# A fused encoder layer: the SSM side chain starts four steps later, loads by SyncE's queue, and its splits stand elsewhere in VectorE's order

## The chip, the cores and the metric

One Trainium2 chip, one core. The metric is the device time of one execution in microseconds, on the slowest core (here the only one). The program is about 19,700 instructions, which each engine executes in the order in which the program was written; between engines there are semaphores.

## The reference, cut to what matters

The kernel computes one layer of a hybrid encoder for an input of 2048 x 1024 floats. The normalised input h is projected once into queries, keys, values, SSM inputs u and the gates of both branches. Branch A is windowed attention. Branch B is a bidirectional state space model: 32 groups of 16 channels with 64 complex states each. Both are projected, gated, summed and added to the input.

```python
h = rms_norm(x, norm_gain[l])
proj = jnp.einsum('bsd,de->bse', h, w_in[l])
q, k, v, z_attn, u_ssm, z_ssm, g = jnp.split(proj, SPLITS, axis=-1)
...
attn = windowed_gqa(q, k, v, attn_sink[l], rel_bias_table) * jax.nn.silu(z_attn)
y = s5_bidirectional(u_ssm, ssm_a_re[l], ssm_a_im[l], ssm_log_dt[l], ...)
...
# in s5_bidirectional, for each direction d:
a_bar = jnp.exp(lam * dt)
_, xs = lax.associative_scan(_scan_op, (a_el, bu), reverse=(d == 1), axis=0)
y = y + Re(xs) c_re - Im(xs) c_im
```

## The kernel before, in words

**Main stream.** TensorE multiplies h with the weights of the input projection, one key (128 output columns) and one block of 512 positions at a time. Numbers are held as a high and a low part, so `mm3` (L220 to L222) issues three matmuls of 128 x 512 for each of eight slices, 24 for one projection. The weights of a key come on SyncE's (SP's) queue into two buffers named raw; `split_w` (L157) has ScalarE round the high part wh (L163) and GpSimd subtract the low part wl in four pieces (L155), which frees the buffer for the next load. The stream goes through 25 keys for blocks 2 and 3, then three keys for all four blocks (there h of blocks 0 and 1 is read again from hS and split by ScalarE, hh L1263, and GpSimd, hl L1267), then 25 keys for blocks 0 and 1.

**Side chain.** Between these matmuls the program places the steps of one generator, `chain` (L1380): the SSM, then attention, then the preparation of the last stage. `turn` (L115) is called four times in a projection and takes as many steps from the chain as a credit allows, 2 x rate for one projection: RATE2 = 1.237 up to the second set of keys, RATE3 = 1.499 behind. So a step of the chain is a place in the order of every engine, some ten projection matmuls long.

**The SSM.** `ssm` (L669) works through eight frames of four groups. Ahead of them the start section (L986 to L1006) loads U, builds the first tables and the first matrices. In each `frame(i)` (L913) the order is fixed by hand, with tables and splits of frame i + 1 placed between steps of frame i:

- `mats` (L783): TensorE transposes the table wt (L796), ScalarE writes Wh (L799), VectorE Wl (L790). wt is made by `prep_w`, on GpSimd (L692 to L694 with `part`), and on VectorE for frame 0; `prep_e` makes the tables ec and es on GpSimd, three products each.
- `zmat` (L804): TensorE forms Z from the negated table wo (L821, negated by ScalarE L760) and writes a last piece (L828); VectorE adds the diagonal (L831). Z is stored to zS and loaded again as M by `load_m` (L838) in another layout; `split_m` splits it (L748 on ScalarE, L749 on VectorE).
- `inject` (L858): TensorE applies W to U, whose two halves come by `load_u` (L773) and are split by `split_u` (L748, L749).
- `rotate` (L867, L868, L870), `scan` (L879), rotate again: VectorE, the recurrence. Then `high_h` (ScalarE, Hh L886) and `low_h` (VectorE, Hl L891) split the state. This happens twice in a frame, for two halves.
- `emit` (L893): TensorE sums M times U (L901) and the table ws times H (L905). ScalarE evacuates Y (L909).
- `prep_o` (L729): the output table wo of the next frame, on VectorE: six operations (L692 to L694).

All loads of U and M are issued by ScalarE's queue (L773, L838), in order with ScalarE's other work.

## Time and profile before

| | us |
|---|---|
| runs of the kernel, median of 3 | 1507.56 (1506.02 to 1509.1) |
| the profiled execution | 1508.19 |
| its span | 1506.4 |
| TensorE busy in the span | 1418.1 (94%) |
| VectorE busy | 1041.8 (69%) |
| ScalarE busy | 659.9 (44%) |
| GpSimd busy | 637.9 (42%) |

The profile is one execution, recorded by the hardware. PE is TensorE, PEld its weight loads, DVE VectorE, ACT ScalarE, POOL GpSimd, SP SyncE; ACTq and SPq are the instructions by which these engines issue DMAs. A matmul's end is modelled, so gaps between starts tell more than durations. The clock that the page gives, PEclk, is the share of full speed granted to TensorE: 1.00 is 2.4 GHz, 0.50 is 1.2 GHz.

### The profile page before, as it was taken

The page shows a single profiled execution, that of the slowest core. Times are in us where ns is not written, and L with a number is a line of the kernel's source. Part 1 is how long each engine was busy: PE and PEld are TensorE (multiplying, and loading weights), DVE is VectorE, ACT ScalarE, POOL GpSimd, SP SyncE. Part 2 cuts the span into 40 slices and gives each one's busy share as a digit, 9 for nine tenths or more (in the row PEclk, how much of TensorE's full clock was granted, in tenths as well). Part 3 has the DMA queues.
Part 4 walks back from the last instruction along what each step waited for, and adds up shares of the span by engine and source line. Part 5 has one row for each costly group of instructions (what it writes and reads, how often), then busy time and mean ns, then how long its engine had stood idle before and what let it go on. Part 6 is the DMA issues. An engine that isn't in the chain of part 4 may idle for free.

```text
span 1506.4 us, 19697 instructions
## 1 busy us (share of the span) xinstructions
PE 1418.1 (94%) x6933; PEld 1154.6 (77%) x6933; DVE 1041.8 (69%) x1954; ACT 659.9 (44%) x1213; POOL 637.9 (42%) x683
## 2 busy tenths in 40 slices
PE   7999779899999999899999999999988999999998
PEld 6787567777778777788888888888766877877886
DVE  2327977779788788647999998874577386385442
ACT  6332133433534444535666666754453243242111
POOL 5520187758678777622111111112376153252320
PEclk9999989989999999999999999999999999999999
DMA  8534222322332332554333333235776375375441
GB/s 264 157 98 95 64 81 72 100 91 76 113 105 88 109 105 88 152 175 127 92 91 92 101 96 91 90 102 148 211 212 193 98 196 181 114 182 166 117 122 70
DMA packets 240723, 185.47 MB, mean 123 GB/s; under 512 B 57921, under 2 KB 202433, under 8 KB 240625
## 3 DMA queue, kind: packets, MB, share of 16 engines
q10 hardware_dynamic: 118192, 107.89, 24.3%
q1 hardware_dynamic: 122432, 76.34, 17.1%
q8 instruction: 54, 0.88, 0.2%
q14 instruction: 45, 0.36, 0.1%
HBM read 126.56 MB, written 57.62 MB: 122 GB/s over the span
## 4 chain that ended last, share of the span: by engine, by line
PE 39%; DVE 26%; issue 7%; DMA 6%; ACT 5%; POOL 4%; ACTq 1%; DVEq 0%; POOLq 0%; SPq 0%
PE pj L220 7%; PE pj L222 7%; PE pj L221 7%; PE s L1592 3%; PE s L1593 3%; PE s L1594 3%; DVE Hl L891 2%; DMA yt<-yS 2%; DVE X L879 2%; PE s L1163 2%; DVE X L868 2%; PE s L1110 2%; DVE rt L867 2%; DVE X L870 2%; PE s L1147 2%
## 5 line engine op out<-in xcount | busy, mean ns | idle before, releaser
L155 POOL TENSOR_TENSOR wl<-raw,wh 128x256 fp32r<-128x256 f32 x380 | 355.0, 964 | 573.5 <-ACT wh L163 483.7
L220 PE MATMUL pj<-hh,wh 128*128 128x512 f32 x976 | 391.2, 401 | 0.0
L222 PE MATMUL pj<-hh,wl 128*128 128x512 f32 x976 | 385.7, 395 | 0.0
L221 PE MATMUL pj<-hl,wh 128*128 128x512 f32 x976 | 385.6, 395 | 0.0
L222 PEld LDWEIGHTS pj<-hh,wl 128*128 128x128 f32 x976 | 185.6, 190 | 41.0
L220 PEld LDWEIGHTS pj<-hh,wh 128*128 128x128 f32 x976 | 186.3, 191 | 34.0
L221 PEld LDWEIGHTS pj<-hl,wh 128*128 128x128 f32 x976 | 186.1, 191 | 34.3
L163 ACT ACTIVATE wh<-raw 128x1024 fp32r<-128x1024 f32 x96 | 100.7, 1051 | 23.4 <-DMA raw<-in_w_branch_ssm_dram 7.9
L1592 PE MATMUL s<-woh,mh 128*128 128x512 f32 x256 | 102.3, 400 | 6.7 <-DVE xr L1599 6.7
L1594 PE MATMUL s<-woh,ml 128*128 128x512 f32 x256 | 102.0, 398 | 0.0
L1593 PE MATMUL s<-wol,mh 128*128 128x512 f32 x256 | 101.9, 398 | 0.0
L1127 ACT ACTIVATE p<-p,sml 128x384 f32<-128x384 f32 (+1 forms) x128 | 75.8, 594 | 16.3 <-DVE sml L1123 16.1
L1636 POOL TENSOR_TENSOR sm<-sm,mhalf 128x1 f32<-128x1 f32 x15 | 8.3, 550 | 170.1 <-DVE sm L1635 133.4
L404 ACT ACTIVATE st<-pj,bg 128x512 f32<-128x512 f32 x64 | 43.8, 685 | 79.0 <-PE pj L222 69.3
L1111 DVE CUSTOM_DVE_ANT_0 p<-s,bias 128x384 f32<-128x384 f32 (+1 forms) x128 | 68.3, 535 | 13.7 <-PE s L1110 13.2
L1599 DVE TENSOR_TENSOR xr<-xr,s 128x512 f32<-128x512 f32 x32 | 21.9, 686 | 69.3 <-PE s L1594 69.3
L867 DVE TENSOR_TENSOR rt<-X,es 128x1020 f32<-128x1020 f32 x32 | 43.3, 1353 | 38.1 <-issue 14.4
L1152 DVE TENSOR_TENSOR pl<-s,ph 128x512 fp32r<-128x512 f32 x92 | 62.9, 683 | 4.2 <-ACT ph L1150 2.9
L1110 PE MATMUL s<-kst,qs 128*128 128x384 f32 (+1 forms) x256 | 65.7, 339 | 0.0
L1592 PEld LDWEIGHTS s<-woh,mh 128*128 128x128 f32 x256 | 48.5, 189 | 20.5 <-DVE xr L1599 8.9
L870 DVE TENSOR_TENSOR X<-X,rt 128x510 f32<-128x510 f32 x64 | 62.0, 1009 | 1.1
L891 DVE TENSOR_TENSOR Hl<-X,Hh 64x1024 fp32r<-64x1024 f32 x32 | 46.7, 1460 | 17.9 <-ACT Hh L886 17.4
(307 smaller groups left out, 3049.2 us busy)
## 6 DMA issues: line engine op xcount, KB each, us to landing
raw<-in_w_in_dram SPq DMA_DIRECT2D x59, 512.0 KB
gS<-st ACTq DMA_DIRECT2D x64, 256.0 KB
gt<-gS ACTq DMA_DIRECT2D x64, 256.0 KB
x<-in_x_dram SPq DMA_DIRECT2D x16, 512.0 KB
raw<-in_w_branch_attn_dram SPq DMA_DIRECT2D x32, 256.0 KB
raw<-in_w_branch_ssm_dram SPq DMA_DIRECT2D x32, 256.0 KB
out_dram<-xr ACTq DMA_DIRECT2D x15, 512.0 KB
xr<-in_x_dram SPq DMA_DIRECT2D x12, 512.0 KB
```

Source lines behind the costliest of these rows:

```text
L155: eng.tensor_tensor(lo[:, ks], r[:, ks], hi[:, ks].bitcast(F32), ALU.subtract)
L163: A.activation(res[0], r, AF.Copy)
L220: PE.matmul(pt, w[0][:, k], r[0][:, k], start=start and k == 0, stop=False)
L221: PE.matmul(pt, w[0][:, k], r[1][:, k], start=False, stop=False)
L222: PE.matmul(pt, w[1][:, k], r[0][:, k], start=False, stop=stop and k == kt - 1)
L870: V.tensor_tensor(X[:, :, r], X[:, :, r], t[:, :, r], ALU.add if r == back else ALU.subtract)
L891: V.tensor_tensor(H[1][rows], xv, H[0][rows].bitcast(F32), ALU.subtract)
L1110: PE.matmul(pt[:, 0:w], s["qs"][:, h], kst[:, r, kv, k0 * 128:k1 * 128], start=r == 0, stop=r == 1)
L1127: A.activation(p[:, h, 0:w], p[:, h, 0:w], AF.Exp, bias=nm[:, j:j + 1], accum_out=den[:, j:j + 1])
L1592: PE.matmul(pt, mh[k][:, ts_], wo[0, n][:, k], start=k == 0, stop=False)
L1593: PE.matmul(pt, mh[k][:, ts_], wo[1, n][:, k], start=False, stop=False)
L1594: PE.matmul(pt, ml[k][:, ts_], wo[0, n][:, k], start=False, stop=k == KD - 1)
```

## The change

The chain waits four steps before it begins, and its start has further yields, so that the first transposes of `mats` come six steps later and the frames seven. U and M are loaded by SP's queue instead of ScalarE's, and M one step earlier. In a frame, M is split right after the first Hl, ahead of the rotation; both halves of the next U are split before the first `emit`, ahead of the second Hl; the six VectorE operations of `prep_o` come in two parts of three in two steps. The rate of the attention is 1.56 instead of 1.499. No arithmetic changes.

```diff
-RATE3 = 1.499
+RATE3 = 1.56
...
-        def prep_o(i, eng=Q):
-            raw_o[i] = [pool.tile(sh, F32, tag=f"wo{n}", name=f"wo{n}") for n in range(2)]
-            table(raw_o[i], i, wo_re, wo_im, cc_re, cc_im, eng)
+        def prep_o(i):
+
+            o = [pool.tile(sh, F32, tag=f"wo{n}", name=f"wo{n}") for n in range(2)]
+            pr, pi, qr, qi = bc(wo_re, i, 1), bc(wo_im, i, 1), bc(cc_re, i, 0), bc(cc_im, i, 0)
+            for n, (a, b, c, d, op) in enumerate(((pr, qr, pi, qi, ALU.subtract), (pr, qi, pi, qr, ALU.add))):
+                r = rtile().rearrange("p g r m -> p g (r m)")
+                t = [r[:, m].rearrange("p (g j c) -> p g j c", g=GB, c=C) for m in range(2)]
+                V.tensor_tensor(t[0], a, b, ALU.mult)
+                V.tensor_tensor(t[1], c, d, ALU.mult)
+                V.tensor_tensor(o[n], t[0], t[1], op)
+                if n == 0:
+                    yield
+            raw_o[i] = o
...
-                A.dma_start(out=raw[:, j], in_=chan(uS, i * GB + half * 2 + j))
+                nc.sync.dma_start(out=raw[:, j], in_=chan(uS, i * GB + half * 2 + j))
...
-                A.dma_start(
+                nc.sync.dma_start(
                     out=raw[:, g],
...
             yield from slot()
+            load_m(i)
             if nx:
                 next(ms)
             split_o(i)
             yield from slot()
-            load_m(i)
             high_h(i, 0)
...
             low_h(i)
+            split_m(i)
             rotate(i, 1, 0)
             yield from slot()
-            split_m(i)
             scan(i, 1)
...
             yield from slot()
+            if nx:
+                split_u(nx, 0)
+                split_u(nx, 1)
             yield from slot()
             yield from emit(i, 0)
...
             if nx:
                 mirror_e(nx, 0)
+                po = prep_o(nx)
+                next(po)
             yield from slot()
             if nx:
-                prep_o(nx, V)
-                split_u(nx, 0)
+                next(po, None)
             yield from slot()
             yield from emit(i, 1)
-            if nx:
-                split_u(nx, 1)
+            st.pop(i)
+            yield from slot()
             if nn:
                 load_u(nn, 0)
                 load_u(nn, 1)
-            st.pop(i)
-            yield from slot()

         raw_o, ph = {}, {}
+        for _ in range(4):
+            yield
         load_u(0, 0)
...
         yield
-        prep_o(0, V)
+        yield
+        yield from prep_o(0)
         yield
         yield from mats(0)
         split_u(0, 0)
         split_u(0, 1)
+        yield
...
-        yield
+        yield from slot()
         for i in range(NB):
             yield from frame(i)
```

The first place is VectorE in the middle of a frame, from the first Hl of the frame on. Line numbers after the change are ten to fourteen higher. This is VectorE before:

```order
L891 TENSOR_TENSOR Hl<-X,Hh 64x1024 x2
L867 TENSOR_TENSOR rt<-X,es 128x4x255
L868 TENSOR_TENSOR X<-X,ec 128x4x255
L870 TENSOR_TENSOR X<-X,rt 128x2x255 x2
L749 TENSOR_TENSOR Ml<-Ml,Mh 128x512
L879 SCALAR_TENSOR_TENSOR X<-rho,X 128x255 x4
```

Ml's split stands here behind the whole rotation.

And this is the same place after the change:

```order
L901 TENSOR_TENSOR Hl<-X,Hh 64x1024 x2
L759 TENSOR_TENSOR Ml<-Ml,Mh 128x512
L877 TENSOR_TENSOR rt<-X,es 128x4x255
L878 TENSOR_TENSOR X<-X,ec 128x4x255
L880 TENSOR_TENSOR X<-X,rt 128x2x255 x2
L889 SCALAR_TENSOR_TENSOR X<-rho,X 128x255 x4
```

The split of M (Ml) has moved from behind the rotation to in front of it, right behind Hl.

The second place is the end of the same frame on VectorE, around the second Hl. This is VectorE before, with the splits of U last:

```order
L891 TENSOR_TENSOR Hl<-X,Hh 64x1024 x2
L692 TENSOR_TENSOR rt<-wo_re,cc_re 128x512
L693 TENSOR_TENSOR rt<-wo_im,cc_im 128x512
L694 TENSOR_TENSOR wo_3916<-rt 128x512
L692 TENSOR_TENSOR rt<-wo_re,cc_im 128x512
L693 TENSOR_TENSOR rt<-wo_im,cc_re 128x512
L694 TENSOR_TENSOR wo_3917<-rt 128x512
L749 TENSOR_TENSOR U0l<-U0l,U0h 128x512
L749 TENSOR_TENSOR U1l<-U1l,U1h 128x512
```

Both splits of U wait here until the table is done.

And this is the same place after the change, with those splits first:

```order
L759 TENSOR_TENSOR U0l<-U0l,U0h 128x512
L759 TENSOR_TENSOR U1l<-U1l,U1h 128x512
L901 TENSOR_TENSOR Hl<-X,Hh 64x1024 x2
L736 TENSOR_TENSOR rt<-wo_re,cc_re 128x512
L737 TENSOR_TENSOR rt<-wo_im,cc_im 128x512
L738 TENSOR_TENSOR wo_4504<-rt 128x512
L736 TENSOR_TENSOR rt<-wo_re,cc_im 128x512
L737 TENSOR_TENSOR rt<-wo_im,cc_re 128x512
L738 TENSOR_TENSOR wo_4505<-rt 128x512
```

The two splits of U stand ahead of Hl instead of behind the six operations of the table; the table's operations themselves are the same.

The third place is SP's queue, which before held weight and h loads alone in this part of the program, after the change in frame 6, where h of blocks 0 and 1 (hS) is read again:

```order
L177 DMA raw_5121<-hS_69 128x1024
L177 DMA raw_5123<-hS_69 128x1024
L783 DMA U0l_5125<-uS_57 128x1x256 x2
L783 DMA U1l_5128<-uS_57 128x1x256 x2
L177 DMA raw_5301<-hS_69 128x1024
L177 DMA raw_5308<-hS_69 128x1024
L848 DMA Ml_5324<-zS_68 128x1x128 x4
L177 DMA raw_5373<-hS_69 128x1024
```

Four loads of h, the loads of U and those of M now stand in one queue, the latter directly behind two loads of h.

## Rows read from the trace of the kernel before

**Rows 1.** The page, line 1: busy us (share of the span) and instructions.
```profile
PE 1418.1 (94%) x6933; PEld 1154.6 (77%) x6933; DVE 1041.8 (69%) x1954; ACT 659.9 (44%) x1213; POOL 637.9 (42%) x683
```

**Rows 2.** Busy time by stretches: window, length, busy us per engine, PEclk, DMA share, GB/s.
```profile
190.00:652.00 462.00, 429.31 (x2369) 352.00 (x2370) 368.01 (x371) 202.51 (x327) 336.04 (x319) 0.96 0.32 99
437.00:607.00 170.00, 163.48 (x932) 134.39 (x930) 138.26 (x137) 77.51 (x124) 128.74 (x119) 1.00 0.32 101
740.00:1000.00 260.00, 257.20 (x1317) 214.41 (x1317) 238.88 (x730) 173.17 (x435) 40.75 (x56) 1.00 0.31 96
```

**Rows 3.** TensorE's waits, 190 to 652 us: us in total, times, longest us.
```profile
PE s L901 <- DVE Ml L749: 11.7, 6, 4.0
PE s L796 <- issue: 11.7, 1, 11.7
PE s L858 <- DVE U0l L749: 7.0, 6, 1.6
PE s L796 <- POOL wt L694: 5.5, 1, 5.5
PE s L821 <- ACT wo L760: 4.0, 1, 4.0
PE s L905 <- DVE Hl L891: 3.7, 2, 3.5
```

**Rows 4.** Busy time by stretches, right behind the first and the last stall.
```profile
190.90:194.00 3.10, 3.10 (x10) 2.51 (x10) 3.03 (x4) 1.02 (x2) 2.94 (x4) 0.50 0.31 100
616.90:620.60 3.70, 3.69 (x19) 2.97 (x20) 2.27 (x2) 2.46 (x5) 3.29 (x4) 0.50 0.93 255
```

**Rows 5.** Timeline at the start (start us, duration, engine, line; in brackets idle time before).
```profile
174.22 0.39 PE L220 MATMUL pj<-hh,wh 128*128 128x512 f32 x1
...
178.30 0.39 PE L220 MATMUL pj<-hh,wh 128*128 128x512 f32 x1
...
190.88 1.08 PE L796 MATMUL s<-ident,wt 128*128 128x128 f32 x4 [11.73 <-issue]
...
187.52 0.42 DVE L441 TENSOR_TENSOR eh_im<-eh_im,tb 128x256 f32<-128x256 f32 x1
...
189.78 0.99 DVE L694 TENSOR_TENSOR wt<-rt 128x512 f32<-128x512 f32 x1
...
190.72 0.60 ACT L396 ACTIVATE st<-pj 128x512 f32<-128x512 f32 x1 [14.88 <-DMA U1l<-uS]
...
188.16 1.04 POOL L692 TENSOR_TENSOR t<-eh_re,el_re 128x256 f32<-128x256 f32 x1 [9.16 <-issue]
...
199.89 1.07 POOL L694 TENSOR_TENSOR es<-t,t 128x256 f32<-128x256 f32 x1
205.12 1.44 POOL L155 TENSOR_TENSOR wl<-raw,wh 128x256 fp32r<-128x256 f32 x2 [4.16 <-ACT wh L163]
```

**Rows 6.** Timeline of frame 4, TensorE and VectorE.
```profile
456.20 0.26 PE L828 MATMUL s<-cc_re,bx_re 128*32 128x16 f32 x8
...
489.10 0.39 PE L905 MATMUL s<-Hl,ws0h 128*128 128x256 f32 x1
...
456.95 0.36 DVE L831 SCALAR_TENSOR_TENSOR Z<-eye,dd,Z 128x16 f32<-128x16 f32 x1 [2.94 <-ACT Z L830]
...
486.14 2.90 DVE L891 TENSOR_TENSOR Hl<-X,Hh 64x1024 fp32r<-64x1024 f32 x2 [1.13 <-ACT Hh L886]
...
495.60 1.21 DVE L749 TENSOR_TENSOR U0l<-U0l,U0h 128x512 fp32r<-128x512 f32 x1
```

**Rows 7.** Who waited for the loads of M (line L838): us, times.
```profile
  ACT Hh L886: 9.6, 6
```

**Rows 8.** Line L868, one instruction form: ns min/median/max, 190 to 650 us.
```profile
L868 DVE TENSOR_TENSOR X<-X,ec x32: 1220/1524/1645, 209.6 to 648.2; 128x1020 f32<-128x1020 f32 x32
```

**Rows 9.** Timeline while h is loaded again.
```profile
592.32 8.48 POOL L1267 TENSOR_TENSOR hl<-raw,hh 128x256 fp32r<-128x256 f32 x8
...
618.30 1.30 DVE L867 TENSOR_TENSOR rt<-X,es 128x1020 f32<-128x1020 f32 x1 [8.90 <-POOL hl L1267]
```

## The prediction

> **What bounds the kernel now.** I read the page's busy times first: TensorE is busy for 1418.1 us, 94% of the span, and VectorE comes next with 69% [rows 1]. So time can only come from the places where TensorE stands still or runs at a lower clock. The next view is the busy time by stretches. In the stretch of the SSM frames, 190 to 652 us, TensorE is busy 429.31 of 462 us at a granted clock of 0.96 (in the quietest frames, 437 to 607 us, 163.48 of 170 at 1.00); in the attention behind them, 740 to 1000 us, it is busy 257.20 of 260 at 1.00 [rows 2]. What the change touches before the end of the frames therefore has room; the attention has hardly any. The view of TensorE's waits names the room: six groups, 17 stalls, 11.7+11.7+7.0+5.5+4.0+3.7 = 43.6 us [rows 3]. Two of them are at the start (L796, the first transposes, and L796 waiting for GpSimd's table), two are splits that VectorE delivers late (Ml, U0l), one is the negated output table of one frame, one is Hl. After seven of these stalls the clock is down; in the first and the last such stretch it stands at 0.50, which is the 1.2 GHz level, for 3.10 and 3.70 us [rows 4], so 1.6 and 1.9 us are lost there, and with the five shorter ones I put the loss at 8.4 us, 1.2 each. The stage loses about 43.6 + 8.4 = 52 us. That is all that this change can win there.
>
> **The start.** TensorE runs projection matmuls to 179.0, and its next instruction, a transpose of the table wt, stands at 190.88, after 11.73 us of nothing [rows 5]. The row names nobody, but VectorE shows the reason: its parameter arithmetic (L441) ends at 187.94, and the first wt is written at 190.77 [rows 5]. The change puts four steps and further yields in front: by the order of instructions the first transposes stand 54 projection matmuls further back. One is 0.227 us (18 of them from 174.22 to 178.30 [rows 5]), so TensorE comes there at 179.0 + 12.3 = 191.3, half a microsecond after the table. I take the stall and its clock loss as gone: 11.7 + 1.6 = 13.3 us. ScalarE's stand of 14.88 us behind the loads of U in its own queue [rows 5] goes too, but it lay beside that stall.
> A new wait appears. GpSimd's twelve prep_e products begin at 188.16, when L441 is done, and end at 200.96 [rows 5]; the third key's low weights stand behind them, as before (the first of four pieces, 1.44/2 = 0.7 us, at 201.7), but TensorE, no longer held up, asks for them 20 matmuls and eight transposes after the first transposes, at 191.3 + 4.5 + 1.2 = 197.0. That is a stall of 4.7 us, and 1.5 of clock; bounds 0, if TensorE is late itself, and 7, if VectorE's table work slows the twelve products by a fifth more than now (12.8 us, so 2.6). The second stall there, L796 behind GpSimd's wt(1), 5.5 + 1.2, has six more steps to be covered, while GpSimd's list grows by one key: I leave 0.5. Start: 20 before, 6.7 after.
>
> **The splits.** Ml's split moves on VectorE from behind rotate(i,1,0) to in front of it, past the rows L867, L868 and L870, of which one takes some 1.5 us [rows 8], so at least 4 us earlier; the stalls behind it, 11.7 us with the longest 4.0 [rows 3], go. U0l and U1l move from behind the six operations of the output table, at 495.60, to in front of the second Hl, which there begins at 486.14 [rows 6]: 9.5 us earlier, against stalls of at most 1.6 [rows 3]. Both go, 18.7 us and about 1.9 of clock. The bounds are 0, if what replaces them waits as long, and 20.6.
>
> **What is late next.** The second Hl. In frame 4 TensorE issues the last Z products at 456.20 and the first product that reads the second Hl at 489.10; Hl is ready at 489.04 [rows 6], just in time. VectorE works from Z (456.95) to there almost without a pause, 1.13 us of waiting for ScalarE's Hh included [rows 6]. The change puts both splits of U, some 2.3 us by the 1.21 of the row [rows 6], in front of this Hl, and the 1.13 us of waiting falls under them. So Hl comes 1.1 to 2.3 us later in such a frame, where there is no slack; other frames had some, since only two of the eight stalled at Hl before [rows 3]. I take 0.7 us for each of frames 3 to 5 (bounds 0 and 2.3) and 0.5 for frame 0. Frame 1 already waited 3.5 us [rows 3]; I take 3 for it, 2 for frame 2, and 0.6 of clock for each.
> Frame 6 lies in the stage in which h is loaded again. There the new order has the load of M on SP behind two loads of h, whose buffers GpSimd frees with eight pieces of hl that take 8.48 us [rows 9]; VectorE already waited 8.90 us behind such pieces in frame 7 [rows 9]. M's split now stands in front of the rotation, so a late M holds VectorE and Hl with it: 4 us and 1.5 of clock (bounds 0 and 8.5). Frame 7 waited 4.0 us, and lost 1.9 of clock, for the table that ScalarE negates. The table's first part is now written a step earlier; I leave 1 (bounds 0 and 5.9).
> Frames after: 0.5 + 3.6 + 2.6 + 2.1 + 5.5 + 1 = 15.3 us, for 32 before.
>
> **Moves without a price.** The eight loads of a frame leave ScalarE's queue. They delayed it: Hh waited 9.6 us behind M's loads in six frames [rows 7]. By the row the move helps Hh, and through it the 1.13 us above; nothing else of TensorE's hung on it.
> The Trainium skill ("Trainium Kernel Development and Optimization", Key Constraints) says that the queues of SP, ScalarE and GpSimd feed the same 16 DMA engines, so that spreading issues saves only issue time. By it the move would be worth nothing on TensorE's path, which is also what the sum takes; the row shows more than issue time, a queue that stood still.
> Two parts of prep_o instead of one change no operation. The attention's rate grows by 1.56/1.499 = 1.041; VectorE is busy 238.88 of 260 us there [rows 2], 92%, which becomes 95.6%. I charge 1.5 us; bounds 0 and 13 (26 units of attention at half a microsecond, the deficit if every one runs VectorE-bound). The attention still ends before the tail needs it.
>
> **Sum.** 52 - (6.7 + 15.3) - 1.5 = 28.5 us less. The profiled execution took 1508.19 us (span 1506.4), 0.6 above the median of 1507.56, so I set the gain against the median: 1479.
>
> **Rivals.**
> *Stalls return at Hl in every frame.* The frames are the same work packed tighter, and VectorE's rotation runs slower while GpSimd works: 1220 ns at best, 1524 in the middle, 1645 at worst for the same instruction [rows 8]. With the frame at the slow end Hl is late by 2.3 + 1.0 + 1.1 = 4.4 us; at some 3 us and 1 of clock in each of eight frames the stage loses 32 + 6.7, a gain of 52 - 38.7 - 1.5 = 12: about 1496. For it: frame 4 is already just in time. Against: in frame 4 most rows were at the slow end already.
> The Trainium skill ("SBUF — State Buffer", Who interferes with whom) has a rule that speaks for this rival: VectorE with two SBUF inputs and a reading GpSimd exclude each other through a shared port, so that one blocks for a whole instruction. The measured step from 1220 to 1645 ns agrees in direction.
> *Attention becomes VectorE-bound* at the higher rate: 13 us instead of 1.5, so 1490. For it: 92% busy. Against: TensorE's idle time there is 2.8 us in 260, with no sign of a limit near.
> *Only the start is won*, the frames exchange one wait for another: 13.3 of the gain stay less 1.5, 1496; or the start's new wait on GpSimd is larger than the old.
> *The other side: M's loads wait on SP in every frame as in frame 6.* SP's queue holds weight loads whose buffers GpSimd frees; ScalarE's queue did not. If M came 5 us late (one set of four pieces behind a busy GpSimd) each frame would lose 5 + 1.5 + 0.7 = 7.2 us, 57.6 in eight, 64 with the start against 52: slower by 12 + 1.5, 1521. It decides from about 4 us of lateness in all frames. For it: in frames 1 and 6 a weight or h load stands directly ahead of M's. Against: in the other six, projection work lies between the two, and a load that could wait has been issued by then.
>
> **How the numbers follow.** A measurement here tells about 0.2%, 3 us, from no change. My forecast has a chance of 0.55, the return at Hl 0.17, the attention 0.10, the start alone 0.10, SP's queue 0.05, an even balance of stalls won and stalls gained 0.03. Faster by over 0.2%: 0.90; within: 0.05 (the return at Hl at its upper end, 45 + 6.7, lands there); slower: 0.05. The range reaches down to all bounds of the new waits near zero in the frames and half at the start (44 us less, 1463) and up past the three middle rivals, 1497.
>
> **What would show it.** Right: no stall before the first transposes, one of 3 to 6 us at L222 for GpSimd's low weights soon after; no waits for Ml and U0l outside frame 6; Hl as the main name in TensorE's list with about ten us; clock 0.98 in the frames. Wrong: Hl above 25 us in total, Ml waits in frames other than 1 and 6, or a busy share of TensorE in the attention below 0.98.

## The result: slower by 0.6%, and the profile after

The changed kernel takes 1515.3 us (median of 6, 1513.39 to 1516.99) against 1506.79 us (median of 6, 1502.15 to 1510.3) for the kernel before. The ratio is 1.0058, with a 95% interval of 1.0045 to 1.0071. So it became slower, where a gain of 28.5 us was forecast. The profiled execution of it has a span of 1515.2 us at a mean clock of 0.986 (before: 1506.4 at 0.979).

The page's line of busy times, after, answers to [rows 1]:

```profile
PE 1416.7 (94%) x6933; PEld 1148.2 (76%) x6933; DVE 1029.7 (68%) x1954; ACT 659.2 (44%) x1213; POOL 632.3 (42%) x683
```

Every engine's busy time is within 1.2% of what it was; what has changed is where the work stands. The busy time by stretches (window and length, then PE, PEld, DVE, ACT, POOL busy, PEclk, DMA share, GB/s) answers to [rows 2]:

```profile
190.00:652.00 462.00, 429.80 (x2405) 351.94 (x2404) 360.99 (x372) 204.97 (x330) 336.02 (x324) 0.97 0.32 101
437.00:607.00 170.00, 156.01 (x877) 126.79 (x877) 129.13 (x129) 77.92 (x123) 123.91 (x121) 0.98 0.34 108
740.00:1000.00 260.00, 249.22 (x1262) 205.59 (x1263) 229.39 (x715) 170.34 (x427) 38.30 (x52) 1.00 0.30 92
```

In the stage of the frames TensorE issues 2405 matmuls in the same 462 us where it issued 2369, at a clock of 0.97 instead of 0.96. But in the attention, which I took as settled, it is busy 249.22 us of 260 where it was 257.20: a share of 0.96, below the 0.98 that was set as a sign of being wrong. TensorE's waits in the stage of the SSM frames (us in total, times, longest) answer to [rows 3]:

```profile
PE s L915 <- DVE Hl L901: 10.7, 7, 3.8
PE pj L222 <- POOL wl L155: 8.4, 3, 4.9
PE pj L221 <- POOL hl L1283: 5.8, 2, 5.6
PE pj L220 <- DVE st L401: 2.2, 1, 2.2
PE s L915 <- ACT Hh L896: 2.2, 1, 2.2
PE s L831 <- ACT wo L770: 2.1, 1, 2.1
PE s L911 <- ACT Mh L758: 0.7, 1, 0.7
PE s L911 <- DVE Ml L759: 0.2, 1, 0.2
```

The start's stall of 11.7 us and the wt stall of 5.5 are gone, Ml is down from 11.7 to 0.2 and U0l has disappeared. Hl is the main name, 10.7 us, and a set of new ones stands beside it: GpSimd's wl and hl, an evacuation (st), Hh.

**Where the 9 us come from.** For all further comparisons I divide the spans into stages and ask how much of each stage TensorE did not use. For every matmul I take the time to the next one's start, subtract the median of that kind in the kernel before, and sum it over a stage, so that a matmul moved from one stage to another doesn't count. The stages: the start up to the last of the second frame's transposes (some 226 us), the frames to the last emit, the opening of the attention up to its first scores, the attention to its last product, the rest. Differences from the kernel before in us; minus is won:

| kernel | start (with what is ahead) | frames | opening | attention | rest | span |
|---|---|---|---|---|---|---|
| the change | -14.1 | -4.2 | +0.1 | +18.9 | +8.2 | +8.8 |
| its forecast | -13.3 | -16.7 | 0 | +1.5 | 0 | -28.5 |

The measured row adds up to the span's 8.8 but for rounding. How far two profiles differ of themselves shows experiment 2: up to 691 us its TensorE executes the same instructions in the same order as before, and yet its start stands at -1.4 and its frames at -2.9. So differences under 3 us in the start and the frames mean nothing in the numbers below. The start came out as forecast. The frames gained little, and the attention and the stage behind it lost 27 us.

### The profile page after: what moved, and what is told of

The parts are those of the page before. It is cut to its first block, busy times and chain, and to the rows that moved or that the text cites. A ratio compares the mean times of both kernels' runs of the same rounds, so it can differ in the third digit from the quotient of the medians.

```text
span 1515.2 us, 19697 instructions
## 1 busy us (share of the span) xinstructions
PE 1416.7 (94%) x6933; PEld 1148.2 (76%) x6933; DVE 1029.7 (68%) x1954; ACT 659.2 (44%) x1213; POOL 632.3 (42%) x683
## 3 DMA queue, kind: packets, MB, share of 16 engines
q1 hardware_dynamic: 131136, 82.63, 18.3%
## 4 chain that ended last, share of the span: by engine, by line
PE 39%; DVE 22%; DMA 8%; issue 6%; ACT 6%; POOL 5%; ACTq 1%; SPq 0%; POOLq 0%; DVEq 0%
PE pj L220 7%; PE pj L222 7%; PE pj L221 7%; PE s L1608 3%; PE s L1609 3%; PE s L1610 3%; DMA yt<-yS 3%; DVE Hl L901 2%; POOL wl L155 2%; PE s L1179 2%; DVE X L889 2%; PE s L868 2%; DVE X L878 2%; DVE rt L877 1%; PE s L1126 1%
## 5 line engine op out<-in xcount | busy, mean ns | idle before, releaser
L220 PEld LDWEIGHTS pj<-hh,wh 128*128 128x128 f32 x976 | 185.2, 190 | 37.3 <-DVE st L401 2.6
L1127 DVE CUSTOM_DVE_ANT_0 p<-s,bias 128x384 f32<-128x384 f32 (+1 forms) x128 | 68.4, 534 | 13.2 <-PE s L1126 12.1
L1166 ACT ACTIVATE ph<-s 128x512 fp32r<-128x512 f32 x92 | 54.3, 590 | 48.6 <-PE s L1163 36.7
```

Source lines behind the costliest of these rows:

```text
L220: PE.matmul(pt, w[0][:, k], r[0][:, k], start=start and k == 0, stop=False)
L1127: V.tensor_tensor_reduce(out=p[:, h, 0:w], in0=pt[:, 0:w], in1=bias[:, kv * 4 + h, r0:r1:-1], scale=1.0, scalar=0.0, op0=ALU.add, op1=ALU. ...
```

## The experiments

Each edit is against the kernel named in its heading or beside it. A ratio is the time over that of the kernel before, run beside it; its median lies between 1506.8 and 1509.3 us in these comparisons, so the ratios are what to compare. Numbers by stages come from one profiled execution each.

### 1. The changed kernel with the old rate

```diff
-RATE3 = 1.56
+RATE3 = 1.499
```

> The changed kernel with RATE3 back at 1.499. Theory 1 (the rate makes the attention wait: 762 projection matmuls stand in it instead of 792, and a unit is then paced by the loop TensorE, VectorE, ScalarE, 9.9 us a unit): TensorE's waits for the attention's VectorE results fall from about 19 us to about 5, 14 to 18 us are won there; only 168 projection matmuls stand behind the attention instead of 210, 9.5 us less cover for the preparation of the last stage, of which up to 10 us come back: about 1507, 1499 to 1510. Theory 2 (the shift of the chain, not the rate, puts the evacuations of the gates in bad places of the units): the attention's waits stay near 19 us, and the time at 1515 or above, up to 1525 with the shorter cover.

Measured: 1500.67 us, ratio 0.9944 (0.9924 to 0.9963). One number of the change, the rate, turns a gain of 0.56% into a loss of 0.58%. By stages it has -16.0 in the start, -4.1 in the frames, -0.2 in the attention and +11.9 in the rest: the attention is as before, and the rest loses about what 54 projection matmuls take (54 x 0.227 = 12.3 us), which no longer stand between the attention and the last stage. Theory 1 holds as to who is to blame: the rate.

### 2. The kernel before with the new rate

```diff
-RATE3 = 1.499
+RATE3 = 1.56
```

> The kernel before with RATE3 1.56 alone. Theory 1 (the rate makes the attention wait): the attention's VectorE waits of TensorE rise from 4.4 us to about 19, 14 to 18 us are lost; the attention ends with 264 projection matmuls behind it instead of 222, which can win back at most 5: 1516 to 1525. Theory 2 (the shift, not the rate): the attention's waits stay below 8 us and the time is 1503 to 1509.

Measured: 1520.92 us, ratio 1.0076 (1.0054 to 1.0097). The rate alone makes the kernel slower by about as much as the whole change. The time lies in theory 1's range, but not for its reasons: in the profiled execution the attention loses 7.0 us instead of 14 to 18, and the rest, which was to win something back with 42 more projection matmuls behind the attention, loses 6.0.

### 3. The later start alone

```diff
         raw_o, ph = {}, {}
+        for _ in range(4):
+            yield
         load_u(0, 0)
...
         yield
+        yield
         prep_o(0, V)
         yield
+        yield
         yield from mats(0)
         split_u(0, 0)
         split_u(0, 1)
+        yield
```

> The kernel before with the later start of the chain alone (four steps of waiting and the further yields; loads stay on ScalarE's queue, splits and rate stay). Theory 1: the start wins its 16 us (the stalls of 11.7 and 5.5 go, one of about 4.9 for GpSimd's low weights comes), frames and attention stay as before, and the attention ends with 168 projection matmuls behind it instead of 222, 12 us less cover, of which 5 to 12 show as waits before the gelu stage: 1495 to 1504. Theory 2 (the shift spoils the attention): attention waits above 12 us, 1506 to 1515.

Measured: 1501.28 us, ratio 0.9944 (0.9924 to 0.9963). Start -12.1, frames -7.9, attention +0.2, rest +12.8. The start's two stalls go (one of 5.0 us for wl comes), and the rest loses 12.8 us in several waits of the last stage's preparation. So waiting in the chain doesn't make work for TensorE: the 54 matmuls that fill the start are missing later. What is left as a gain, 7 us, is about what the frames gained; which of their waits the other place in the stream shortened was not tried.

### 4. The moved splits alone

```diff
+            load_m(i)
             if nx:
                 next(ms)
             split_o(i)
             yield from slot()
-            load_m(i)
             high_h(i, 0)
...
             low_h(i)
+            split_m(i)
             rotate(i, 1, 0)
             yield from slot()
-            split_m(i)
             scan(i, 1)
...
             yield from slot()
+            if nx:
+                split_u(nx, 0)
+                split_u(nx, 1)
             yield from slot()
             yield from emit(i, 0)
...
                 prep_o(nx, V)
-                split_u(nx, 0)
             yield from slot()
             yield from emit(i, 1)
-            if nx:
-                split_u(nx, 1)
```

> The kernel before with the moved splits alone (M's load a step earlier and its split ahead of the rotation, both splits of U ahead of the first emit; ScalarE's queue, output table in one part, start and rate as before). If the splits are worth what the waits for Ml and U0l were and Hl takes only a part back: those 18.7 us go, Hl rises from 3.7 to about 11, net 8 to 12 us, 1495 to 1500. If the frames exchange one wait for another, as the changed kernel's trace suggests: 1503 to 1509, Hl at 12 or more, or new waits for ScalarE's Mh behind the loads in its queue.

Measured: 1509.29 us, ratio 1.0006 (0.9992 to 1.0020): no change. TensorE's waits in the frames (226 to 661 us) of this kernel:

```profile
PE s L905 <- DVE Hl L891: 12.1, 5, 3.1
PE pj L220 <- DVE st L401: 5.6, 2, 3.8
PE s L821 <- ACT wo L760: 4.4, 1, 4.4
PE pj L222 <- POOL wl L155: 1.9, 1, 1.9
```

Ml and U0l, 17.8 us before in this window, have gone, and 18.9 us have taken their place: Hl up from 3.7 to 12.1, an evacuation that VectorE does late (st, 5.6), wl 1.9, Y 1.6, Hh 1.0, and 0.4 more for wo. The frames exchanged one set of waits for another of the same size.

### 5. The rate lowered

```diff
-RATE3 = 1.499
+RATE3 = 1.44
```

> The kernel before with RATE3 lowered to 1.44. At 1.499 each unit of the attention holds exactly 24 projection matmuls; at 1.56 some hold 18, at 1.44 some hold 30. Theory pace (a higher rate leaves TensorE too few matmuls for the loop through VectorE): with more matmuls between, TensorE's waits in the attention fall below before's 3 us and its units that hold 24 matmuls take 9.5 to 10 us as before. Theory step (1.499 keeps units and projections in step, and any other rate lets them drift into worse positions): units of 24 matmuls take up to 11 us here too, and TensorE loses 5 us or more in the attention, as at 1.56. With 186 matmuls behind the attention instead of 222 the tail loses 3 to 8 us under both: pace 1509 to 1516, step 1514 to 1525.

Measured: 1534.52 us, ratio 1.0177 (1.0163 to 1.0192), above both ranges. The attention lost 11.2 us and the rest 15.4, of which only 3 to 8 had been set for the rest. A lower rate gives TensorE more matmuls in the attention, and it waits there more, not less. The attention's windows (busy time by stretches, from the first score matmul to the last product), of the kernel before:

```profile
698.00:1014.00 316.00, 313.05 (x1600) 261.33 (x1600) 284.28 (x872) 208.56 (x524) 49.80 (x68) 1.00 0.31 94
```

of the changed kernel:

```profile
689.00:1017.00 328.00, 312.16 (x1570) 257.43 (x1570) 280.36 (x871) 207.61 (x522) 47.10 (x64) 0.99 0.30 89
```

of the changed kernel at 1.499:

```profile
690.00:1006.00 316.00, 311.12 (x1601) 263.04 (x1600) 283.16 (x871) 206.83 (x525) 55.90 (x68) 1.00 0.32 96
```

of the kernel before at 1.56:

```profile
691.00:1007.00 316.00, 307.94 (x1568) 256.21 (x1569) 279.18 (x873) 206.14 (x521) 49.06 (x64) 1.00 0.30 92
```

and at 1.44:

```profile
699.00:1033.00 334.00, 323.00 (x1631) 268.18 (x1630) 283.10 (x872) 210.10 (x527) 51.36 (x68) 0.99 0.30 92
```

At 1.499 the stretch takes 316 us, in the old and in the new place. At 1.56 in the kernel before it takes 316 us as well, with 30 projection matmuls fewer in it (762 instead of 792 by the order of instructions, 6.8 us of work). At 1.44 it takes 334 us with 30 more, where 6.8 would be their due. In the changed kernel it takes 328 us with 30 fewer. Where it is lost shows in the distances from one unit's first score matmul to the next, and the projection matmuls counted between them (second to thirteenth unit, from the timeline; a unit is 128 positions and one key head; there are 32):

```
before 1.499   us   8.9  9.6 10.1  9.7 10.0  9.6 10.1  9.6 10.1  9.6 10.1  9.7
               pj    24   24   24   24   24   24   24   24   24   24   24   24
before 1.44    us   9.5 10.2 12.0 10.7 10.7 10.7  9.6  9.8 11.3 11.9 10.9 14.7
               pj    24   24   30   24   24   24   24   24   30   24   24   24
changed 1.56   us   9.4 11.2 14.4 11.1 12.2  8.2 10.5 10.8 10.8  9.6 11.1  9.3
               pj    24   24   24   24   24   18   24   24   24   24   24   18
changed 1.499  us   9.4 10.7  9.6 10.7  9.6  9.7  9.6 10.7  9.6 10.7  9.6 10.7
               pj    24   24   24   24   24   24   24   24   24   24   24   24
```

At 1.499 the chain takes 2.998 steps in one projection, three in practice, and a unit of the attention is three steps: each unit holds exactly one projection's matmuls, and nearly all take 9.6 to 10.7 us. At 1.56 (3.12 steps) and 1.44 (2.88) units and projections slide past each other. A unit with 18 matmuls between is then quick, 8.2 us, but units with the same 24 take up to 14.4 in the changed kernel and 14.7 at 1.44. The theory of pace fell, since a lower rate would have had to help; that of step fits all four kernels.

### 6. The loads on SP's queue alone

```diff
-                A.dma_start(out=raw[:, j], in_=chan(uS, i * GB + half * 2 + j))
+                nc.sync.dma_start(out=raw[:, j], in_=chan(uS, i * GB + half * 2 + j))
...
-                A.dma_start(
+                nc.sync.dma_start(
                     out=raw[:, g],
```

> The kernel before with the loads of U and M on SP's queue alone. If the queue is off TensorE's path: Hh comes earlier on ScalarE, M and U land as before, 1504 to 1510. If SP's order (loads of M behind weight and h loads that wait for GpSimd) is what ate the splits' gain: 1512 to 1520 with TensorE waiting for M, or for GpSimd's hl in the stage in which h is read again.

Measured: 1497.78 us, ratio 0.9937 (0.9920 to 0.9953): below both ranges. It is worth about as much as the later start alone, and I had given it no price. TensorE's waits in its frames (226 to 661 us):

```profile
PE s L858 <- DVE U0l L749: 8.0, 5, 2.1
...
PE s L901 <- DVE Ml L749: 4.5, 5, 2.1
```

The wait for Ml fell from 11.7 to 4.5 us though its split stands where it stood. Frames -8.0, start -3.0 (1.5 of it before 48 us, ahead of everything that was moved), attention +0.6, rest -0.4.

### 7. The splits with U behind the second Hl

```diff
-            if nx:
-                split_u(nx, 0)
-                split_u(nx, 1)
             yield from slot()
             yield from emit(i, 0)
...
             low_h(i)
             if nx:
+                split_u(nx, 0)
+                split_u(nx, 1)
                 mirror_e(nx, 0)
```

(against experiment 4).

> The kernel with the moved splits alone, but with both splits of U right behind the second Hl, ahead of the output table, instead of ahead of that Hl. If the 2.3 us in front of Hl were the exchange: Ml's 11.7 and U0l's 7.0 stay away, Hl falls back from 12.1 to about 4, and 10 to 15 us are won: 1493 to 1499. If VectorE and GpSimd have no slack in the frames whatever stands first: other waits fill in (the evacuations L401, the table) and the time is 1502 to 1509.

Measured: 1502.16 us, ratio 0.9963 (0.9947 to 0.9979). Frames -9.5. TensorE's waits there:

```profile
PE s L821 <- ACT wo L760: 7.4, 2, 6.1
PE s L905 <- DVE Hl L891: 5.9, 4, 1.5
PE pj L220 <- DVE st L401: 5.8, 2, 3.8
```

Hl halves to 5.9, Ml and U0l stay away, the late evacuation (5.8) and the negated table (up from 4.0 to 7.4) remain, and below these lines stands the 5.4 for wt that the kernel before has too. So U's place ahead of Hl was part of the exchange, and the gain is at the edge between the two expectations.

### 8. The later start with a shorter opening of the attention

```diff
         kv_load(2)
-        for _ in range(4):
-            yield
+        yield
...
             yield
-            yield
+            if n == 3:
+                yield
             if n >= 2:
```

(against experiment 3).

> The kernel before with the later start alone, and with six empty steps taken out of the attention's opening (loads of k and v), two projections' worth, so that units and projections stand in the same step. If the later start's only price is the shorter cover of the last stage (168 matmuls; with this edit 216): the start's 16 us stay, the tail's 12 us come back, 1488 to 1496. If the opening needs those steps (VectorE and ScalarE stand behind the loads of k and v, and the evacuations behind them): 1500 to 1508, with new waits between 650 and 700 us.

Measured: 1506.98 us, ratio 0.9986 (0.9977 to 0.9996), worse than without. The first score matmul now stands still, with its engine's idle time in brackets:

```profile
685.50 0.98 PE L1115 MATMUL s<-kst,qs 128*128 128x384 f32 x2 [6.78 <-issue]
```

Opening +7.0, attention +3.2, rest +9.0 instead of +12.8. The empty steps of the opening were needed. And of the 54 matmuls that the later start took from behind the attention 48 stand there again (216, before 222), but the rest won back only 3.8 of its 12.8 us: cover alone doesn't set what it loses.

### 9 to 11. Start and queue together, and what can be added

The later start with SP's queue and the rate 1.499 (the edits of experiments 3 and 6):

> The kernel before with the later start and SP's queue, splits, output table and rate (1.499) as before. If the two gains are of different places and add: 7.5 + 9.4 us, 1489 to 1495, with frames as in the run with SP's queue alone and the tail as in the run with the start alone. If the loads of U, now behind other weights on SP, or the later frames undo SP's gain: 1497 to 1503, as the changed kernel at 1.499.

Measured: 1497.41 us, ratio 0.9923 (0.9911 to 0.9935). The two gains don't add up in full: frames -11.3 where the start alone had -7.9 and the queue alone -8.0.

The same with the splits of experiment 7 (the edits of 3, 6, 4 and 7):

> As the run with the later start and SP's queue, and M split ahead of the rotation, both halves of U behind the second Hl and ahead of the table. If the splits' waits (Ml, U0l) are real losses: another 4 to 8 us less than without, 1483 to 1490. If early splits of M hold VectorE's queue when M's load is late (SP's queue behind loads of h): 1492 to 1500 with TensorE waiting for GpSimd's hl near 590 us.

Measured: 1493.26 us, ratio 0.9898 (0.9882 to 0.9913), frames -15.9, the most of all runs. The time lies in the second range, but not for its reason: TensorE doesn't wait for hl.

The first one with three steps of the opening taken out:

```diff
         kv_load(2)
-        for _ in range(4):
-            yield
+        yield
```

> As the run with the later start and SP's queue, and three of the empty steps taken out of the attention's opening, one projection's worth: 192 matmuls behind the attention instead of 168, 5.4 us more cover. If six steps were too many only because of the last three: 3 to 5 us less than without. If the first three already uncover the loads of k and v: no gain or up to 5 us more, with waits between 650 and 700 us.

Measured: 1497.83 us, ratio 0.9931 (0.9918 to 0.9943): nothing won, 2.7 us of new waits in the opening and 1.5 in the attention for about 5 in the rest.

### 12. The changed kernel at 1.499 with M on ScalarE's queue

```diff
-                nc.sync.dma_start(
+                A.dma_start(
                     out=raw[:, g],
```

(in `load_m`, against experiment 1.)

> The changed kernel at rate 1.499 with M's loads back on ScalarE's queue, U's loads on SP's. If M's loads behind two loads of h on SP hold M's early split, through it VectorE's rotation, GpSimd's next table and hl: the 5.6 us wait for hl and the 1.1 us for M go, 5 to 9 us less than the 1500.7 of the kernel with 1.499: 1491 to 1497. If ScalarE's queue holds Hh behind the loads of M as before and that weighs more: 1499 to 1506. If hl waits for another reason: its 5.6 us stay.

Measured: 1509.02 us, ratio 0.9998 (0.9987 to 1.0009), so 8 us slower than with SP, and above all ranges. ScalarE stands behind M's loads in its own queue (ScalarE's waits, 230 to 660 us):

```profile
ACT Wh L809 <- DMA Ml<-zS: 16.4, 7, 3.9
```

The load stands a step earlier here than in the kernel before, ahead of Wh instead of Hh, and holds 16.4 us of ScalarE's time instead of 9.6 [rows 7]. The wait for hl shrinks only from 5.6 to 4.5 us. Yet VectorE's split of M, which stood still for 6.93 us in frame 6 of the changed kernel, stands still for 0.46 us here. So the place of M's load on SP isn't what makes hl late.

### 13. The changed kernel at 1.499 with U behind the second Hl

```diff
             yield from slot()
-            if nx:
-                split_u(nx, 0)
-                split_u(nx, 1)
             yield from slot()
             yield from emit(i, 0)
...
             if nx:
+                split_u(nx, 0)
+                split_u(nx, 1)
                 mirror_e(nx, 0)
```

> The changed kernel at rate 1.499 with both splits of U right behind the second Hl instead of ahead of it; the output table stays in two parts behind them. If the place ahead of Hl is what the frames lost: Hl's waits fall from 10.8 us to 7 or 8, the 5.6 us wait for hl goes, 1491 to 1496. If the table in two parts or the later load of U is to blame: 1498 to 1503, as the changed kernel at 1.499.

Measured: 1498.24 us, ratio 0.9933 (0.9920 to 0.9946), 2.4 us less than experiment 1, but the two intervals overlap, so no gain is shown. Hl falls from 10.8 to 8.2, the wait for hl stays at 5.2.

### 14. The best version at 1.56

```diff
-RATE3 = 1.499
+RATE3 = 1.56
```

(against the version of 1493.26 us.)

> The version with the later start, SP's queue, M split early and U behind the second Hl (1493.3) at rate 1.56. If the price of 1.56 is set by where units and projections stand (the chain reaches the attention at the same places as in the changed kernel): 15 to 20 us lost in the attention, 4 won back in the tail, 1503 to 1511. If the changed kernel's 18.5 came from its frames: 7 us in the attention, 1496 to 1501.

Measured: 1508.56 us, ratio 0.9995 (0.9980 to 1.0010). Attention +17.2, rest +9.0, frames -14.3, as without to within the noise. This is nearly the changed kernel's 18.9 again, with other frames but with the chain at the same place in the stream. The attention's window:

```profile
681.00:1008.00 327.00, 311.26 (x1571) 257.58 (x1572) 280.70 (x872) 207.69 (x522) 48.05 (x65) 0.99 0.30 90
```

327 us, beside the 328 of the changed kernel; the kernel before at the same rate, whose chain is 54 matmuls earlier, had 316. What 1.56 costs depends on where the units meet the projections.

### 15. GpSimd's order at the start

```diff
         prep_w(0, V)
+        yield
         prep_e(0, 0)
         prep_e(0, 1)
         drain_work()
         yield
-        yield
         prep_o(0, V)
```

(against the version of 1493.26 us.)

> The same version at 1.499 with the twelve prep_e products one step later, so that the third key's low weights stand ahead of them on GpSimd. If the stall of 4.9 us near 200 us is GpSimd's order alone: it goes with its clock loss, 5 to 6.5 us less than 1493.3: 1486.5 to 1489. If the tables are needed as soon as they are made, or the fourth key's weights now wait in the same place: 1491 to 1496.

Measured: 1487.06 us, ratio 0.9861 (0.9845 to 0.9877): the fastest kernel here, 21 us faster than the kernel before beside it and some 28 faster than the change. On GpSimd the third key's low weights now run in the time in which it had nothing to do:

```profile
184.66 3.26 POOL L155 TENSOR_TENSOR wl<-raw,wh 128x256 fp32r<-128x256 f32 x4 [7.38 <-ACT wh L163]
188.42 1.05 POOL L692 TENSOR_TENSOR t<-eh_re,el_re 128x256 f32<-128x256 f32 x1 [0.51 <-POOL wl L155]
```

The 4.9 us wait for them has gone. The largest name left from 190 to 661 us is Hl:

```profile
PE s L905 <- DVE Hl L891: 8.0, 6, 3.4
```

### 16 and 17. The two edits left

Between the version of 1493.26 us and experiment 13 stand the table in two parts, a later load of U and, at the end of the start section, `yield from slot()` in place of `yield`, by which GpSimd's work comes in another order (see below, on frame 6). The table in two parts, alone (with `prep_o` as in the change):

```diff
                 mirror_e(nx, 0)
+                po = prep_o(nx)
+                next(po)
             yield from slot()
             if nx:
-                prep_o(nx, V)
+                next(po, None)
```

> The version at 1493.3 with the output table in two parts alone. If the first part, right behind the second Hl and a step earlier, is what costs: 1496 to 1500, with TensorE's wait of about 5 us for hl back near 590 us. If not: 1491 to 1495, no wait for hl.

Measured: 1494.7 us, ratio 0.9897 (0.9870 to 0.9924). No wait for hl; the parts cost nothing that can be told within this wide interval.

The later load of U, alone:

```diff
             yield from emit(i, 1)
-            if nn:
-                load_u(nn, 0)
-                load_u(nn, 1)
             st.pop(i)
             yield from slot()
+            if nn:
+                load_u(nn, 0)
+                load_u(nn, 1)
```

> The version at 1493.3 with the load of the U after next one step later alone. If it is this that puts the loads of h and M one behind the other on SP: 1496 to 1500 with the wait for hl back. If not: 1491 to 1495, no wait for hl.

Measured: 1498.06 us, ratio 0.9926 (0.9906 to 0.9945). No wait for hl either. The frames stand at -9.4 instead of -15.9, but the intervals of the two ratios touch (0.9906 and 0.9913), so that the later load of U costs something, some 4 us, is likely and not shown. The wait for hl comes with neither edit; the third was not run alone.

## Why the prediction was wrong, point by point

**The start: right.** The first transposes come at 191.30 us (forecast 191.3) without a stall, and TensorE then waits for the third key's low weights (wl). The timeline of the changed kernel:

```profile
201.06 3.00 POOL L155 TENSOR_TENSOR wl<-raw,wh 128x256 fp32r<-128x256 f32 x3
...
191.30 0.60 PE L806 MATMUL s<-ident,wt 128*128 128x128 f32 x4
...
201.84 0.80 PE L222 MATMUL pj<-hh,wl 128*128 128x512 f32 x1 [4.87 <-POOL wl L155]
```

4.87 us, against 4.7 forecast and with the cause named. The wt stall, for which 0.5 was left, is gone. The stage won 14.1 us, the forecast was 13.3.

**The frames: Hl right in its total, the sum wrong.** Hl was forecast at "about ten us" and is 10.7; per frame it is 1.1 to 1.7 in frames 1 to 4, where 0.7 to 3 were set, but 3.75 in frame 0, for which 0.5 was set, so that the total fits in part by luck. Ml and U0l went. What failed is the step that put nothing for any other wait: two waits for wl around 540 us (3.5), an evacuation that VectorE does behind its splits (2.2), Hh (2.2), the table (2.1) and hl (5.8) came in, 15.8 us, where 1 us was set, for the table. Experiment 4 shows it for the splits without the other edits: 17.8 us of waits left, 18.9 came. The rival in which only the start is won described this.

**Frame 6: M late as forecast, the wait another one.** 5.5 us were set for a late M behind the loads of h, holding VectorE and then Hl. The timeline of the changed kernel:

```profile
573.36 0.33 SPq L177 DMA_DIRECT2D raw<-hS  x1
...
573.84 2.47 SPq L848 DMA_DIRECT2D Ml<-zS  x4
...
575.26 2.82 POOL L1283 TENSOR_TENSOR hl<-raw,hh 128x256 fp32r<-128x256 f32 x4
...
579.00 0.63 ACT L758 ACTIVATE Mh<-Ml 128x512 fp32r<-128x512 f32 x1 [5.62 <-DMA Ml<-zS]
...
579.66 0.69 DVE L759 TENSOR_TENSOR Ml<-Ml,Mh 128x512 fp32r<-128x512 f32 x1 [6.93 <-ACT Mh L758]
...
589.34 0.88 POOL L694 TENSOR_TENSOR ec<-t,t 128x256 f32<-128x256 f32 x1 [10.10 <-DVE X L878]
...
592.53 0.80 PE L221 MATMUL pj<-hl,wh 128*128 128x512 f32 x1 [5.61 <-POOL hl L1283]
```

SP issues M's loads right behind a load of h; M's split on ScalarE waits 5.62 us for them and VectorE 6.93, as forecast. But TensorE meets little of it, 0.9 us for M and 0.7 for Hl. What it meets is hl, 5.61 us: GpSimd runs the four pieces of one load of h at 575.26, then its next table (ec), which waits 10.10 us until VectorE has read the old one, and the pieces of the following loads stand behind that table. That the sum lies near the 5.5 that were set is luck.

The order of GpSimd's instructions tells where this comes from. In experiment 17 M is as late (ScalarE waits 4.87 us for it, VectorE 6.78), but there the four pieces of the next load run ahead of the table too, and TensorE doesn't wait for hl:

```profile
575.29 2.82 POOL L1271 TENSOR_TENSOR hl<-raw,hh 128x256 fp32r<-128x256 f32 x4
581.10 4.81 POOL L1271 TENSOR_TENSOR hl<-raw,hh 128x256 fp32r<-128x256 f32 x4 [2.98 <-ACT hh L1267]
...
591.62 1.18 POOL L694 TENSOR_TENSOR ec<-t,t 128x256 f32<-128x256 f32 x1 [3.78 <-DVE X L868]
```

The diff's last lines hold what differs: ahead of the frames `yield` became `yield from slot()`. `slot` takes an item off GpSimd's list of tables at every second call (or when more than three are waiting), so one call more moves that list against everything else, in all frames. The four kernels with this line (the change, experiments 1, 12 and 13) have the table ahead of those four pieces, and all wait for hl, 4.5 to 5.6 us at once, and for wl near 540 us, 2.1 to 3.5 in all. No kernel without it has either wait there, and the edits of experiments 16 and 17 leave GpSimd's order as it is. So a late M is neither needed for the wait (experiment 12) nor enough (experiment 17); this order is what the kernels with it share. The line wasn't run alone, so its price isn't measured; in experiment 17 TensorE waits 3.3 us for Hh and Hl in this place instead.

**The queue: wrong.** "Moves without a price" was the step, and "nothing else of TensorE's hung on it". Experiment 6 gives the move alone 0.63%, experiment 12 gives 8 us in the changed kernel. The rows that told it were there: Hh had waited 9.6 us [rows 7], ScalarE 14.88 [rows 5], and on ScalarE stand U's and M's high parts and evacuations too: in experiment 6 TensorE waited 7.2 us less for the low part of M, though its split stayed in its place. The Trainium skill's sentence ("Trainium Kernel Development and Optimization", Key Constraints), that issuing from several engines saves only issue time, gives the move only that time. The issues of M's loads in the kernel before (ns min/median/max, first and last start):

```profile
L838 ACTq DMA_DIRECT2D Ml<-zS x32: 581/582/630, 231.0 to 633.2; - x32
```

32 issues of 0.58 us are 19 us of ScalarE's time, and U's 32 as much again. Beside them stand its waits, 9.6 us before Hh, which reads no M, and 16.4 before Wh in experiment 12: ScalarE stood behind loads in its own queue that could not go yet. Issue time is one part of the price here, the queue's standing the other; how the 0.63% divide between them isn't shown.

**The attention: the step that failed most.** "I charge 1.5 us; bounds 0 and 13" came from VectorE's share of 92% growing to 95.6. It cost 18.9 us, beyond the bound (which counts 26 units; with all 32 it is 16 us), and VectorE's share fell, to 229.39 of 260. TensorE's waits in the attention, before (698 to 1014 us):

```profile
PE s L1163 <- DVE pl L1152: 2.1, 10, 0.4
PE s L1163 <- DVE ob L1179: 0.4, 1, 0.4
```

and after (689 to 1017 us):

```profile
PE s L1179 <- DVE ob L1195: 7.0, 6, 2.6
PE s L1179 <- DVE pl L1168: 5.3, 9, 1.0
PE s L1163 <- DVE p L1155: 3.3, 8, 0.8
```

15.6 us for VectorE's results where there were 2.5. Behind the longest of these waits (2.59 us, at 727.78) the granted clock stands at 0.50, the 1.2 GHz level, for 3.4 us, so 1.7 us more; the other 4 of the 18.9 stand in no wait of this view. VectorE in turn stands behind an evacuation of the main stream, a projection's product with ScalarE's tanh (th). Its waits for that, in the same two windows, before and after:

```profile
DVE st L401 <- ACT th L400: 2.4, 7, 0.5
DVE st L401 <- ACT th L400: 12.1, 12, 1.4
```

They are 2.1 us in experiment 1, 6.8 in experiment 2, 11.2 in experiment 5 and 11.8 in experiment 14: small at 1.499 in both places of the chain, large where the rate is another. This points to evacuations of the projections that come at bad places of the units. The rival of a VectorE-bound attention had the right place, and a price of 13 us, but not the mechanism: not a full engine but units and projections that no longer run in step (experiments 2, 5 and 14). The row against which I argued, 2.8 us idle in 260, was the mark of a rate tuned to that step. That the step is the whole of it is argued from these rows; no run moved the evacuations alone.

**The rest: a term that was missing.** "The attention still ends before the tail needs it" was the step. By the order of instructions only 12 matmuls fewer stand behind the attention, but the attention ended 3 us later, and the preparation of the last stage with it. ScalarE then waits 6.06 us for the load of what the attention wrote (aS), and TensorE behind it for the evacuation:

```profile
1073.43 0.63 ACT L1500 ACTIVATE ah<-ar 128x512 fp32r<-128x512 f32 x1 [6.06 <-DMA ar<-aS]
1073.96 0.67 ACT L404 ACTIVATE st<-pj,bg 128x512 f32<-128x512 f32 x1
...
1074.68 0.80 PE L220 MATMUL pj<-gh,wh 128*128 128x512 f32 x1 [5.70 <-ACT st L404]
```

The same wait in the kernel before:

```profile
1071.80 0.50 PE L220 MATMUL pj<-gh,wh 128*128 128x512 f32 x1 [1.73 <-ACT st L404]
```

This wait names 4.0 of the 8.2 us. At 1.499 the rest pays 11.9 (experiment 1), at 1.56 the attention pays 18.9 and the rest still 8.2. Cover is not all that sets it: with 264 matmuls behind the attention (experiment 2) the rest lost 6.0, with 216 (experiment 8) 9.0, where the kernel before has 222. What else does stays open.

**The sum.** One term of the 52 us was too small. [rows 4] shows only the first part of two stretches at the lower clock; behind the last stall it goes on to 622.7, and behind frame 1's wait for Hl it lasts 6 us:

```profile
616.90:622.70 5.80, 5.79 (x37) 4.09 (x38) 4.33 (x6) 3.15 (x6) 3.29 (x4) 0.50 0.84 218
319.80:325.80 6.00, 5.97 (x21) 5.39 (x22) 5.89 (x6) 0.61 (x2) 5.92 (x6) 0.50 0.30 86
```

The seven stretches hold 32 us of TensorE's work at 0.50, so by the same halving 16 us are lost and not 8.4. In the changed kernel four such stretches hold 16.7 us, 8.4 lost. Waits down from 43.6 to 32.3 and clock from 16 to 8.4 make 18.9 us; start and frames won 18.3.

Of the forecast's -28.5: start 0.8 better, frames 12.5 worse, attention 17.4 worse, rest 8.2 worse, which is 37.3, as much as the span differs from the forecast.

## What to carry to other kernels

Where a side stream is woven into a main stream at a fixed rate, ask first whether its period and the main stream's are in step, and treat a rate as a number tuned to that step: in the kernel before, 4% up cost 12 us and 4% down cost 26, while the engine that seemed to be the limit had 8% left. Matmuls that are put ahead of a side chain are missing behind it, so look at what the chain feeds at its end before you delay its beginning. Keep loads that wait for their data off the queue of an engine whose compute others wait for. And compare the order of every engine before and after: one line that looked like an empty step moved GpSimd's tables in all frames.

## What the runs showed of the hardware

A load on ScalarE's queue whose data or buffer isn't ready yet holds ScalarE's computation behind it, for 14.88 us at one place; the same loads on SP, whose queue has nothing to compute, made the program 0.63% faster with no other edit. Order alone on an engine that stood idle was worth about 6 us: in experiment 15 GpSimd's four pieces of low weights took 3.26 us from 184.66, while the products that had stood ahead of them began only at 188.16 [rows 5].

VectorE and GpSimd slow each other in the kernel before. Of the 32 instructions of L868 [rows 8] the 11 that run beside no more than 0.1 us of GpSimd's work take 1220 to 1223 ns, the 21 others 1521 to 1645; GpSimd's products of 128x256 (L692 to L694) take 614 to 741 ns where VectorE is idle, and 1062 in the middle beside it.
